# The second half's convolution taps without TensorE, and with only TensorE in the text's order

## The chip, the cores and the metric

One core of a Trainium2 chip runs the whole program. The metric is the time of one execution on the device in microseconds, the median of three runs: 2355.17 us (2353.74 to 2355.51) for the kernel before. The profile comes from one more execution with the profiler on, which took 2358.65 us. The engines are TensorE (PE), VectorE (DVE), ScalarE (ACT), GpSimd (POOL) and SyncE (SP), which issues the DMAs.

## What is computed

Two layers on an input of 1024 positions by 1024 channels. The first layer's mixer is attention, the second's is a Conformer convolution module; behind each mixer comes a feed-forward network with a short convolution (width 3). The change touches the Conformer module, whose core in the reference is:

```
u = h @ w_pw1 + b_pw1
a, g = jnp.split(u, 2, axis=-1)
u = a * jax.nn.sigmoid(g)
u = causal_dwconv(u, w_dw) + b_dw        # 31 taps, each channel by itself
u = rms_norm(u, ln_g)
u = jax.nn.silu(u)
return u @ w_pw2 + b_pw2
```

Each channel has 31 tap weights, and each output position is the sum of 31 shifted products.

## The kernel before

The module runs in two halves of 512 positions, h = 0 and 1. A half has eight tiles `ct` of 128 channels; channels lie across the partitions. All large products are three matmuls on a high and a low part of each operand (`whi`, `wlo` for weights, `hthi`, `htlo` for activations; lines 354 to 356), so each weight block that is loaded (`raw`) is split first: ScalarE makes `whi`, GpSimd or VectorE `wlo`.

For a tile, `glu` (line 1122) gives four weight pieces of 12 matmuls into two PSUM banks (`pw`); then `gate` makes `sg` on ScalarE and `u` on VectorE. `u` has two buffers of 30 + 512 columns. `taps_of` (line 1169) sums the taps:

- ScalarE multiplies the windows of the first `N_POOL` = 10 taps (`pacc`, then nine `prod`), and GpSimd adds them into `pacc`;
- VectorE takes the other taps one after the other into a PSUM tile `cacc` (line 1191), 21 of them;
- `end` adds both into `y` (line 1203). `square` then adds y squared into `sqa` (ScalarE and GpSimd).

In the second half, tiles 4, 5 and 6 (`PE_TILES`) are different: behind their `gate`, `on_pe` (line 1159) has ScalarE make four diagonal matrices `dg` from the tap weights, and TensorE multiplies them with windows of `u` in full float32 (line 1167). So four taps of these tiles are in `cacc` before VectorE begins, and VectorE takes 17.

`first` (line 1219) interleaves this: between groups of three taps it gives out pieces that hold matmuls, by a count (`beat`, `GATES`, `BEAT`) of how much VectorE work has gone out. Such pieces are the next tile's `glu` and fillers. In the second half the fillers are first `rest0`, the closing product of the first half (`dn` sums), with a norm of its four blocks of rows `turned` into the stream (ScalarE squares, GpSimd `ss`, VectorE `hn`, TensorE transposes `nps`, ScalarE `hthi`, VectorE `htlo`), and then `T.early` (`first = T.early(1, keep1, w_up)`), parts of the next up projection (`e` sums, each stored through a copy `ev` on ScalarE).

PSUM has six banks of the pool `up` for `pw`, `dn`, `e` and these `nps`, and two of the pool `t` for `cacc`, column sums and others.

When the taps of the half are done, `norm` (`squares`, `spread`) takes the column sums `ssps` of `sqa` on TensorE, makes the root on GpSimd (`r`), a diagonal `dg` on VectorE and spreads it with a matmul `rb`; then each `y` is scaled, goes through Silu, is split and feeds the closing product `dn`.

The order within an engine is either that of the program's text or one that a scheduler chooses before the program is built, with each instruction's place fixed from then on: every engine works through its own queue in order and waits at its head. `T.order` (line 236) opens a region; with no argument all engines are in the text's order, with `T.order(PE)` TensorE alone is, and the scheduler places the others. Before the change, `T.order()` without argument holds from the end of the first up projection to the start of the second.

Of the kernel before, what the change touches and what calls it, by code (L numbers as in the profile page):

```python
# [9 lines left out]
F32 = mybir.dt.float32  # L10
F32R = mybir.dt.float32r
BF16 = mybir.dt.bfloat16
AF = mybir.ActivationFunctionType
# [4 lines left out]
P = 128  # L18
# [31 lines left out]

N_POOL = 10
ROW_BUFS = 8
PE_TAPS = 4
PE_TILES = (4, 5, 6)
GATES = (2, 1)
BEAT = (3.3, 3.6)
LAG = 3
# [57 lines left out]
class Trunk:  # L115
# [993 lines left out]
    def conv(self, xs, xd, h, ht, w_pw1, los, taps, vec, w_pw2, halo, after):  # L1109


        nc = self.nc
        C = taps.shape[1]
        H = C - 1
        n_pool = N_POOL
        wv = w_pw1.rearrange("(k p) n -> p k n", p=P)
        st = {}
        us = {}
        ys = {}
        accs = {}  # L1120

        def glu(ct):
            pss = [None, None]
# [29 lines left out]
                for q in range(2):  # L1153
                    yield piece(s, q)
            yield Piece(gate, vector=1)
            if h == 1 and ct in PE_TILES:
                yield Piece(lambda: on_pe(ct))

        def on_pe(ct):

            dg = self.part("dg")
            acc = accs[ct] = self.pst.tile([P, 512], F32, tag="t", name=self.n("cacc"))
            for i in range(PE_TAPS):
                j = n_pool + i
                d = dg[:, i * P : (i + 1) * P]
                nc.scalar.activation(d, self.ident, AF.Copy, scale=taps[:, j, ct : ct + 1])
                nc.tensor.matmul(acc, d, us[ct][:, j : j + 512], start=i == 0, stop=i == PE_TAPS - 1)  # L1167

        def taps_of(ct):
            begun = h == 1 and ct in PE_TILES  # L1170
            own = n_pool + (PE_TAPS if begun else 0)
            nv = C - own
            t = {}
            tap = lambda j: taps[:, j, ct : ct + 1]

            def some(i0, i1):
                if i0 == 0:
                    t["u"] = us.pop(ct)
                    t["acc"] = accs.pop(ct) if begun else self.pst.tile([P, 512], F32, tag="t", name=self.n("cacc"))
                    t["pacc"] = self.part("pacc")  # L1180
                    t["done"] = 0
                u, acc, pacc = t["u"], t["acc"], t["pacc"]
                win = lambda j: u[:, j : j + 512]
                if i0 == 0:
                    nc.scalar.activation(pacc, win(0), AF.Identity, bias=vec[:, 2, ct : ct + 1], scale=tap(0))
                for i in range(i0, i1):
                    j = own + i
                    if i == 0 and not begun:
                        nc.vector.tensor_scalar(acc, win(j), tap(j), None, op0=ALU.mult)
                    else:  # L1190
                        nc.vector.scalar_tensor_tensor(acc, win(j), tap(j), acc, op0=ALU.mult, op1=ALU.add)  # L1191
                    while t["done"] < min(n_pool - 1, (n_pool - 1) * (i + 1) // (nv - 2)):
                        t["done"] += 1
                        p = self.part("prod")
                        nc.scalar.activation(p, win(t["done"]), AF.Copy, scale=tap(t["done"]))  # L1195
                        nc.gpsimd.tensor_tensor(pacc, pacc, p, op=ALU.add)  # L1196
# [117 lines left out]
def trunk(ctx, tc, a):  # L1314
    nc = tc.nc
    T = Trunk(ctx, tc)
# [28 lines left out]
    taps, vec = tabs[2]  # L1345
# [165 lines left out]
    def conv(h):  # L1511
        return T.conv(xs, xds[1], h, hc, w_pw1, pwlo, taps, vec, a["conv_w_pw2"][0], halo,
                      normer(grows, keep1, True))
# [4 lines left out]
    PE = mybir.EngineType.PE  # L1518

    def pieces():  # L1520
# [20 lines left out]
        yield from down1  # L1541
        yield from turned(rest0)
        main1, norm1, rest1 = conv(1)
        fill = [rest0]
        main1 = main1(fill)
        yield fetch(grows, a["ffn_norm_g"][1])
# [6 lines left out]
        first = T.early(1, keep1, w_up)  # L1553
        fill.append(first)
        yield from main1
        keep1["vector"] = True
        yield from some(first, 5)
        yield from some(norm1, 1)
# [17 lines left out]
        for d in downs:  # L1576
            yield from d

    T.trace(pieces())


# [23 lines left out]
```

## Time and profile before

| what | us |
|---|---|
| median of three runs | 2355.17 |
| profiled execution | 2358.65 |
| its span | 2356.9 |
| TensorE busy | 2270.7 (96%) |
| VectorE busy | 1648.0 (70%) |
| ScalarE busy | 1359.7 (58%) |
| GpSimd busy | 1402.2 (59%) |

The slices of the profile show the whole span in 40 parts; the second half's taps lie from about 1481 to 1674 us. Busy shares are means over stages with different limits, so the windows, the waits and the timeline of that stretch are to be read. An instruction is named by its line, output and inputs; `cacc<-u,dg` is a tap on TensorE, `cacc<-u,ctaps,cacc` one on VectorE.

### The profile page before, as it was taken

The numbers are of one execution on the slowest core, as the hardware profiler recorded it, in microseconds if no ns is written. First come the engines' busy times: TensorE is split into PE (matmuls) and PEld (weight loads), VectorE is DVE, ScalarE is ACT, GpSimd is POOL, SyncE is SP. The second block draws the span as 40 slices with busy tenths as digits, with TensorE's granted clock in tenths as the row PEclk, the third lists the DMA queues.
The fourth block names the chain that finished last, engine by engine and source line by source line (L and its number), as shares of the span: only waits on it lengthen the run. The fifth ranks groups of instructions, "written<-read, shape, count | busy, mean of one in ns | idle before, by whom it ended". The sixth has DMA issues, their size and how long they took to land.

```text
span 2356.9 us, 35332 instructions
## 1 busy us (share of the span) xinstructions
PE 2270.7 (96%) x11306; PEld 1934.8 (82%) x11306; DVE 1648.0 (70%) x2740; ACT 1359.7 (58%) x2844; POOL 1402.2 (59%) x1187
## 2 busy tenths in 40 slices
PE   7899999999999999999999999978999999999998
PEld 7899999997878887778778887856787888888887
DVE  5577777777378999997337985885738999993222
ACT  5566666666255666666455665555635666664443
POOL 3445545444018988884454895765634999965543
PEclk9999999998999999999999999999999999999999
DMA  4222322143155556666888777533555545466664
GB/s 144 64 79 79 81 77 77 57 166 131 69 176 184 155 161 213 200 198 200 285 273 291 235 251 264 176 110 112 183 180 170 155 152 156 153 220 208 216 206 155
DMA packets 366842, 392.64 MB, mean 167 GB/s; under 512 B 26416, under 2 KB 245312, under 8 KB 366656
## 3 DMA queue, kind: packets, MB, share of 16 engines
q1 hardware_dynamic: 366656, 390.38, 52.1%
q8 instruction: 89, 1.46, 0.2%
q14 instruction: 97, 0.79, 0.1%
HBM read 299.78 MB, written 82.12 MB: 162 GB/s over the span
## 4 chain that ended last, share of the span: by engine, by line
PE 44%; DVE 18%; issue 5%; ACT 3%; DMA 2%; POOL 2%; SPq 0%; DVEq 0%; ACTq 0%; POOLq 0%
DVE acc L580 9%; PE dn L355 7%; PE dn L356 7%; PE dn L354 7%; PE pw L354 2%; PE pw L356 2%; PE pw L355 2%; DVE cacc L1191 2%; PE e L356 1%; PE e L354 1%; PE e L355 1%; ACT acc L584 1%; PE y L354 1%; PE y L355 1%; PE y L356 1%
## 5 line engine op out<-in xcount | busy, mean ns | idle before, releaser
L349 POOL TENSOR_TENSOR wlo<-raw,whi 128x512 fp32r<-128x512 f32 (+1 forms) x305 | 443.0, 1454 | 270.1 <-ACT whi L348 237.2
L348 ACT CAST whi<-raw 128x512 fp32r<-128x512 f32 (+2 forms) x497 | 302.7, 633 | 248.3 <-PE dn L355 159.2
L349 DVE TENSOR_TENSOR wlo<-raw,whi 128x512 fp32r<-128x512 f32 (+1 forms) x192 | 149.5, 783 | 236.8 <-ACT whi L348 221.3
L349 POOL TENSOR_TENSOR wlo<-s,whi 128x512 fp32r<-128x512 f32 x176 | 258.7, 1480 | 66.8 <-ACT whi L348 66.6
L354 PE MATMUL dn<-whi,whi 128*128 128x512 f32 x704 | 276.1, 392 | 1.8 <-ACT whi L348 1.3
L355 PE MATMUL dn<-wlo,whi 128*128 128x512 f32 x704 | 275.2, 391 | 0.9 <-POOL wlo L349 0.9
L356 PE MATMUL dn<-whi,wlo 128*128 128x512 f32 x704 | 275.3, 391 | 0.0
L1191 DVE SCALAR_TENSOR_TENSOR cacc<-u,ctaps,cacc 128x512 f32<-128x512 f32 x311 | 235.0, 756 | 21.9 <-PE cacc L1167 11.5
L1196 POOL TENSOR_TENSOR pacc<-pacc,prod 128x512 f32<-128x512 f32 x144 | 190.1, 1320 | 87.2 <-ACT prod L1195 80.7
L354 PE MATMUL y<-bhi,whi 128*128 128x512 f32 x528 | 207.2, 392 | 6.6 <-DVE u L638 5.2
L356 PE MATMUL y<-bhi,wlo 128*128 128x512 f32 x528 | 205.6, 389 | 0.0
L355 PE MATMUL y<-blo,whi 128*128 128x512 f32 x528 | 205.5, 389 | 0.0
L171 POOL TENSOR_SCALAR ss<-ss 128x4 f32<-128x4 f32 (+1 forms) x96 | 22.8, 238 | 298.5 <-ACT hn L191 156.3
L354 PE MATMUL pj<-whi,hthi 128*128 128x384 f32 (+1 forms) x512 | 178.1, 349 | 5.3 <-DVE zf L824 3.6
L356 PE MATMUL pj<-whi,htlo 128*128 128x384 f32 (+1 forms) x512 | 177.5, 347 | 0.0
L355 PE MATMUL pj<-wlo,hthi 128*128 128x384 f32 (+1 forms) x512 | 176.5, 345 | 0.7 <-DVE wlo L349 0.7
L914 POOL TENSOR_SCALAR x<-x,nm 128x896 f32<-128x896 f32 (+7 forms) x128 | 101.0, 794 | 107.0 <-DVE nm L913 75.3
L558 POOL TENSOR_TENSOR s<-raw,raw 128x512 f32<-128x512 f32 x88 | 124.6, 1416 | 63.7 <-DMA raw<-in_ffn_w_up_dram 35.7
L354 PEld LDWEIGHTS dn<-whi,whi 128*128 128x128 f32 x704 | 132.9, 189 | 30.3 <-ACT whi L348 1.7
L355 PEld LDWEIGHTS dn<-wlo,whi 128*128 128x128 f32 x704 | 132.9, 189 | 29.1 <-POOL wlo L349 1.2
L356 PEld LDWEIGHTS dn<-whi,wlo 128*128 128x128 f32 x704 | 132.9, 189 | 27.6
L584 ACT ACTIVATE acc<-acc 128x512 f32<-128x512 f32 x88 | 55.7, 633 | 166.2 <-DVE acc L580 164.9
(224 smaller groups left out, 6442.8 us busy)
## 6 DMA issues: line engine op xcount, KB each, us to landing
raw<-in_ffn_w_up_dram SPq DMA_DIRECT2D x240, 256.0 KB
raw<-in_ffn_w_down_dram SPq DMA_DIRECT2D x176, 256.0 KB
raw<-actd SPq DMA_DIRECT2D x152, 256.0 KB
raw<-in_conv_w_pw_dram SPq DMA_DIRECT2D x96, 256.0 KB
actd<-acc SPq DMA_DIRECT2D x76, 256.0 KB
wlo<-pwlo SPq DMA_DIRECT2D x64, 256.0 KB
raw<-in_fox_w_in_dram SPq DMA_DIRECT2D x64, 192.0 KB
xd<-x SPq DMA_DIRECT2D x24, 512.0 KB
```

The costliest lines, as they stand in the source:

```text
L171: nc.gpsimd.tensor_scalar(ss, ss, 1.0 / n, EPS, op0=ALU.mult, op1=ALU.add)
L348: self.nc.scalar.copy(hi, raw)
L349: (self.nc.vector if vector else self.nc.gpsimd).tensor_tensor(lo, raw, f32(hi), op=ALU.subtract)
L354: nc.tensor.matmul(out, lh, rh, start=start, stop=False, skip_group_check=more)
L355: nc.tensor.matmul(out, lh, rl, start=False, stop=False, skip_group_check=more)
L356: nc.tensor.matmul(out, ll, rh, start=False, stop=stop, skip_group_check=more)
L558: nc.gpsimd.tensor_tensor(st[o], *(st[m].rearrange("p a b -> p (a b)") if m[0] == "a" else st[m] for m in ((y, x) if o == "s4" else (x, y) ...
L580: nc.vector.scalar_tensor_tensor(acc[:, j:], ps[:, : 512 - j], tap[2 - j], acc[:, j:], op0=ALU.mult, op1=ALU.add)
L584: nc.scalar.activation(acc, acc, AF.Silu)
L914: nc.gpsimd.tensor_scalar(X[:, :L], X[:, :L], nm[:, 2:3], 1.0, op0=ALU.mult, op1=ALU.mult)
L1191: nc.vector.scalar_tensor_tensor(acc, win(j), tap(j), acc, op0=ALU.mult, op1=ALU.add)
L1196: nc.gpsimd.tensor_tensor(pacc, pacc, p, op=ALU.add)
```

## The change

`on_pe` is taken out with its two constants, so every tile of both halves has 21 taps on VectorE and ten on ScalarE and GpSimd. And a region `T.order(PE)` is opened ahead of the second half's taps and closed with `T.order()` behind them: within it only TensorE keeps the text's order.

```diff
--- before.py
+++ after.py
@@ -50,8 +50,6 @@
 
 N_POOL = 10
 ROW_BUFS = 8
-PE_TAPS = 4
-PE_TILES = (4, 5, 6)
 GATES = (2, 1)
 BEAT = (3.3, 3.6)
 LAG = 3
@@ -1117,7 +1115,6 @@
         st = {}
         us = {}
         ys = {}
-        accs = {}
 
         def glu(ct):
             pss = [None, None]
@@ -1153,30 +1150,16 @@
                 for q in range(2):
                     yield piece(s, q)
             yield Piece(gate, vector=1)
-            if h == 1 and ct in PE_TILES:
-                yield Piece(lambda: on_pe(ct))
-
-        def on_pe(ct):
-
-            dg = self.part("dg")
-            acc = accs[ct] = self.pst.tile([P, 512], F32, tag="t", name=self.n("cacc"))
-            for i in range(PE_TAPS):
-                j = n_pool + i
-                d = dg[:, i * P : (i + 1) * P]
-                nc.scalar.activation(d, self.ident, AF.Copy, scale=taps[:, j, ct : ct + 1])
-                nc.tensor.matmul(acc, d, us[ct][:, j : j + 512], start=i == 0, stop=i == PE_TAPS - 1)
 
         def taps_of(ct):
-            begun = h == 1 and ct in PE_TILES
-            own = n_pool + (PE_TAPS if begun else 0)
-            nv = C - own
+            nv = C - n_pool
             t = {}
             tap = lambda j: taps[:, j, ct : ct + 1]
 
             def some(i0, i1):
                 if i0 == 0:
                     t["u"] = us.pop(ct)
-                    t["acc"] = accs.pop(ct) if begun else self.pst.tile([P, 512], F32, tag="t", name=self.n("cacc"))
+                    t["acc"] = self.pst.tile([P, 512], F32, tag="t", name=self.n("cacc"))
                     t["pacc"] = self.part("pacc")
                     t["done"] = 0
                 u, acc, pacc = t["u"], t["acc"], t["pacc"]
@@ -1184,8 +1167,8 @@
                 if i0 == 0:
                     nc.scalar.activation(pacc, win(0), AF.Identity, bias=vec[:, 2, ct : ct + 1], scale=tap(0))
                 for i in range(i0, i1):
-                    j = own + i
-                    if i == 0 and not begun:
+                    j = n_pool + i
+                    if i == 0:
                         nc.vector.tensor_scalar(acc, win(j), tap(j), None, op0=ALU.mult)
                     else:
                         nc.vector.scalar_tensor_tensor(acc, win(j), tap(j), acc, op0=ALU.mult, op1=ALU.add)
@@ -1541,6 +1524,7 @@
         yield from down1
         yield from turned(rest0)
         main1, norm1, rest1 = conv(1)
+        yield T.order(PE)
         fill = [rest0]
         main1 = main1(fill)
         yield fetch(grows, a["ffn_norm_g"][1])
@@ -1553,6 +1537,7 @@
         first = T.early(1, keep1, w_up)
         fill.append(first)
         yield from main1
+        yield T.order()
         keep1["vector"] = True
         yield from some(first, 5)
         yield from some(norm1, 1)
```

What this does to the queues, in rows of the built programs. In VectorE's queue before, where the norm's first rows come (`cacc_17486` and `u_17483` are tile 3, `u_17631` is tile 4, `nps` and `htlo` the first two blocks of the norm):

```order
L436 TENSOR_TENSOR x_16632<-x_16632,dn_17036 128x512
L1191 SCALAR_TENSOR_TENSOR cacc_17486<-u_17483,ctaps,cacc_17486 128x512 x15
L201 SCALAR_TENSOR_TENSOR hn_17556<-x_16629,ss_17555,rows_16833 128x512
L201 SCALAR_TENSOR_TENSOR hn_17556<-x_16629,ss_17555,rows_16835 128x512
L1145 SCALAR_TENSOR_TENSOR u_17631<-pw_3605_17503,cvec,sg_17629 128x512
L323 TENSOR_TENSOR htlo_3603_17498<-nps_17644,hthi_3601_17496 128x4x128
L323 TENSOR_TENSOR htlo_3604_17499<-nps_17651,hthi_3602_17497 128x4x128
L201 SCALAR_TENSOR_TENSOR hn_17625<-x_16629,ss_17624,rows_16833 128x512
L201 SCALAR_TENSOR_TENSOR hn_17625<-x_16629,ss_17624,rows_16835 128x512
L1191 SCALAR_TENSOR_TENSOR cacc_17486<-u_17483,ctaps,cacc_17486 128x512 x3
L1203 TENSOR_TENSOR y_17085<-cacc_17486,pacc_17487 128x512
```

The same place after (`cacc_17301` is tile 2, `u_17486` and `cacc_17489` tile 3):

```order
L434 TENSOR_TENSOR x_16632<-x_16632,dn_17039 128x512
L199 SCALAR_TENSOR_TENSOR hn_17559<-x_16629,ss_17558,rows_16836 128x512
L199 SCALAR_TENSOR_TENSOR hn_17559<-x_16629,ss_17558,rows_16838 128x512
L1174 SCALAR_TENSOR_TENSOR cacc_17301<-u_17280,ctaps,cacc_17301 128x512
L199 SCALAR_TENSOR_TENSOR hn_17628<-x_16629,ss_17627,rows_16836 128x512
L199 SCALAR_TENSOR_TENSOR hn_17628<-x_16629,ss_17627,rows_16838 128x512
L199 SCALAR_TENSOR_TENSOR hn_17661<-x_16632,ss_17660,rows_16836 128x512
L199 SCALAR_TENSOR_TENSOR hn_17661<-x_16632,ss_17660,rows_16838 128x512
L1174 SCALAR_TENSOR_TENSOR cacc_17301<-u_17280,ctaps,cacc_17301 128x512
L199 SCALAR_TENSOR_TENSOR hn_17661<-x_16632,ss_17702,rows_16836 128x512
L199 SCALAR_TENSOR_TENSOR hn_17661<-x_16632,ss_17702,rows_16838 128x512
L1142 SCALAR_TENSOR_TENSOR u_17486<-pw_3564_17310,cvec,sg_17484 128x512
```

The instructions `hn` of all four blocks now stand among the last taps of tile 2 and ahead of `u` of tile 3; before, they stood behind 15 taps of tile 3, and the later three each behind the transposes of the block before.

In TensorE's queue before, behind the last product `pw` of tile 4:

```order
L355 MATMUL pw_3619_17569<-htlo_3417_16564,whi_17432 128x512
L356 MATMUL pw_3619_17569<-hthi_3415_16562,wlo_17433 128x512
L1167 MATMUL cacc_17635<-u_17631,dg_17634 128x512 x4
L210 MATMUL nps_17644<-ident,hn_17556 128x128 x4
L210 MATMUL nps_17651<-ident,hn_17556 128x128 x4
L210 MATMUL nps_17673<-ident,hn_17625 128x128 x4
L210 MATMUL nps_17680<-ident,hn_17625 128x128 x4
L354 MATMUL pw_3643_17694<-hthi_3414_16561,whi_17456 128x512
```

And after:

```order
L353 MATMUL pw_3619_17572<-htlo_3417_16564,whi_17435 128x512
L354 MATMUL pw_3619_17572<-hthi_3415_16562,wlo_17436 128x512
L208 MATMUL nps_17643<-ident,hn_17559 128x128 x4
L208 MATMUL nps_17650<-ident,hn_17559 128x128 x4
L352 MATMUL pw_3638_17666<-hthi_3414_16561,whi_17459 128x512
```

The four tap matmuls are gone, the transposes of the first block follow the `pw` at once, and the 12 `pw` matmuls that begin in the last row stand before those of the second.

In ScalarE's queue after, where tile 5 begins (`sg_17861`, `u_17863`, `pacc_17918` are tile 5, `u_17634` is tile 4, `ev` frees a bank of an `e` sum):

```order
L1139 ACTIVATE sg_17861<-pw_3658_17779,cvec 128x512
L521 COPY ev_17879<-e_3677_17866 128x512
L1178 ACTIVATE prod_17889<-u_17634,ctaps 128x512
L521 COPY ev_17907<-e_3683_17894 128x512
L1168 ACTIVATE pacc_17918<-u_17863,cvec,ctaps 128x512
L1178 ACTIVATE prod_17923<-u_17863,ctaps 128x512
L1141 COPY u_18113<-halo 128x30
L98 CAST whi_17997<-raw_17731 128x512
L521 COPY ev_17938<-e_3669_17834 128x512
L1178 ACTIVATE prod_17949<-u_17863,ctaps 128x512
L1178 ACTIVATE prod_17974<-u_17863,ctaps 128x512
L1178 ACTIVATE prod_17979<-u_17863,ctaps 128x512
```

The second `ev` of `e_3669` stands behind `pacc_17918`, which reads `u_17863`. In this order products of two tiles follow each other, and copies `ev` stand among them. Besides, two `e` pieces (24 matmuls) of the up projection stand among the taps or before the closing product that stood in the second up projection before: the count in `first` gives out more fillers, since VectorE has more taps.

## Rows read from the trace of the kernel before

**Rows 1.** Windows: us; busy of PE, PEld, DVE, ACT, POOL; granted clock; DMA; GB/s.

```profile
1450.00:1555.00 105.00, 96.85 (x438) 78.62 (x436) 86.04 (x120) 63.21 (x114) 69.04 (x58) 1.00 0.58 193
1555.00:1640.00 85.00, 65.32 (x250) 46.19 (x251) 55.50 (x74) 41.52 (x78) 42.78 (x36) 0.90 0.34 112
1640.00:1720.00 80.00, 76.97 (x331) 62.10 (x330) 50.70 (x67) 45.53 (x80) 53.05 (x40) 0.98 0.60 194
...
1700.00:1720.00 20.00, 18.08 (x71) 14.21 (x71) 5.61 (x9) 10.69 (x19) 10.51 (x9) 0.91 0.70 247
```

**Rows 2.** Waits of TensorE, 1430 to 1740: us in total, times, longest.

```profile
PE cacc L1167 <- DVE u L1145: 16.5, 3, 8.2
PE nps L210 <- DVE hn L201: 9.7, 6, 2.2
```

**Rows 3.** Window of line 1167 alone: PE busy, weight loads, clock, DMA, GB/s.

```profile
1540.00:1640.00 100.00, 16.70 (x24) 6.49 (x24) 0.91 0.32 105
```

**Rows 4.** Waits of VectorE, 1481.5 to 1674.2, as rows 2.

```profile
DVE u L1145 <- ACT sg L1142: 13.8, 2, 12.8
DVE cacc L1191 <- PE cacc L1167: 11.5, 2, 5.9
DVE htlo L323 <- ACT hthi L322: 6.8, 1, 6.8
DVE y L1203 <- POOL pacc L1196: 6.0, 3, 3.9
DVE wlo L349 <- ACT whi L348: 5.7, 2, 3.4
```

**Rows 5.** Timeline of VectorE in the taps: start, us, instruction, count.

```profile
1503.03 15.80 DVE L1191 SCALAR_TENSOR_TENSOR cacc<-u,ctaps,cacc 128x512 f32<-128x512 f32 x20
...
1544.79 11.84 DVE L1191 SCALAR_TENSOR_TENSOR cacc<-u,ctaps,cacc 128x512 f32<-128x512 f32 x15
```

**Rows 6.** Timeline of TensorE: start, us, instruction, count, [idle before and what ended it].

```profile
1558.77 5.61 PE L1167 MATMUL cacc<-u,dg 128*128 128x512 f32 x8 [8.24 <-DVE u L1145]
...
1567.48 1.32 PE L210 MATMUL nps<-ident,hn 128*128 128x128 f32 x8 [2.22 <-DVE hn L201]
...
1681.24 0.49 PE L354 MATMUL e<-hthi,whi 128*128 128x512 f32 x1
...
1689.55 1.02 PE L1265 MATMUL rb<-dg,ones 128*128 128x512 f32 x2
...
1697.14 0.50 PE L354 MATMUL dn<-whi,hthi 128*128 128x512 f32 x1 [1.11 <-ACT hthi L1273]
```

**Rows 7.** Window of VectorE alone: busy us (instructions), clock, DMA, GB/s.

```profile
1481.00:1674.14 193.14, 156.54 (x208) 0.96 0.41 130
```

**Rows 8.** Timeline of VectorE around the last tap.

```profile
1672.85 0.68 DVE L349 TENSOR_TENSOR wlo<-raw,whi 128x512 fp32r<-128x512 f32 x1
1673.45 0.69 DVE L1203 TENSOR_TENSOR y<-cacc,pacc 128x512 f32<-128x512 f32 x1
1675.83 4.54 DVE L349 TENSOR_TENSOR wlo<-raw,whi 128x512 fp32r<-128x512 f32 x3 [1.69 <-ACT whi L348]
```

**Rows 9.** Timeline of GpSimd behind the last tap.

```profile
1674.88 1.29 POOL L1217 TENSOR_TENSOR sqa<-sqa,sq 128x512 f32<-128x512 f32 x1 [5.88 <-ACT sq L1216]
...
1676.82 1.30 POOL L558 TENSOR_TENSOR s<-raw,raw 128x512 f32<-128x512 f32 x1 [0.65 <-DVE wlo L349]
...
1684.52 1.29 POOL L349 TENSOR_TENSOR wlo<-s,whi 128x512 fp32r<-128x512 f32 x1
```

**Rows 10.** Timeline of VectorE at the start of the up projection.

```profile
1819.64 0.69 DVE L628 TENSOR_TENSOR u<-y,p 128x512 f32<-128x512 f32 x1 [3.33 <-PE y L356]
```

**Rows 11.** Three tiles, 1481.5 to 1674.2: count, ns min/median/max, first and last start.

```profile
L349 DVE TENSOR_TENSOR wlo<-raw,whi x12: 683/1018/1418, 1589.4 to 1672.9; 128x512 fp32r<-128x512 f32 x12
...
L201 DVE SCALAR_TENSOR_TENSOR hn<-x,ss,rows x8: 737/756/1755, 1556.5 to 1579.6; 128x512 f32<-128x512 f32 x8
...
L1191 DVE SCALAR_TENSOR_TENSOR cacc<-u,ctaps,cacc x151: 742/756/757, 1482.6 to 1672.2; 128x512 f32<-128x512 f32 x151
```

## The prediction

> **What bounds the kernel now.** I began with the windows around the second half's taps [rows 1]. The reader is to see that TensorE is busy nearly all of 1450 to 1555 us, then only 65.32 of the 85 us from 1555 to 1640, at a granted clock of 0.90, and again nearly all of the time to 1720. VectorE is at 86.04 of 105 us in the first stretch and at 55.50 of 85 in the second: there both engines wait. The waits of TensorE [rows 2] name two lines: its tap matmuls wait 16.5 us for `u`, and the transposes `nps` wait 9.7 us for `hn`. Both `u` and `hn` come from VectorE. The tap matmuls themselves take 16.70 us [rows 3]. VectorE waits in turn [rows 4]: 11.5 us for those tap matmuls, 6.8 us for `hthi`, which is made from the transposes that stand behind them, 6.0 us for the adds of GpSimd (`pacc`), 5.7 us for `whi` from ScalarE, 1.0 us for `sg` (the other 12.8 of that row is the wait before the stage). So the two engines hold each other in turns, and neither is the bound alone. The order explains why: in the text's order 15 taps (11.84 us) stand on VectorE before the first `hn` and the next `u` [rows 5], while TensorE has been idle for 8.24 us [rows 6].
>
> **The change on VectorE.** From the start of the first `u` to the end of the last `y` are 193.14 us with 208 instructions [rows 7]. The waits of rows 4 in it are 11.5 + 6.8 + 6.0 + 5.7 + 1.0 = 31.0 us. The change gives VectorE 12 taps more, four for each of tiles 4, 5 and 6. Twenty taps take 15.80 us [rows 5], 0.79 each with the gap, so 9.5 us. With no wait left the stage would take 193.1 - 31.0 + 9.5 = 171.6 us, and the last `y` would end 21.5 us earlier, at 1652.6.
>
> Which waits go? The 11.5 us go with the matmuls. The 6.8 us go too: the order puts the eight `hn` in front of `u` of tile 3, so that the transposes find their inputs when TensorE comes to them. That is 18.3 us. The other 12.7 (`pacc`, `whi`, `sg`) depend on how the scheduler has ordered ScalarE and GpSimd; the bounds are that all stay or none. Going through the queues, I find the products of a tile on ScalarE well ahead of the `y` that needs them, with one place that is tight: the `pacc` of tile 5 waits on ScalarE for `u` of tile 5 and has a product of tile 4 just before it. I keep 3 us. The last `y` then ends at 1655.6, 18.5 us earlier; the bounds are 8.8 and 21.5.
>
> **The change on TensorE.** It loses 16.70 us of tap matmuls and, by the above, most of the 26.2 us of waits in rows 2. In the order of after, 384 matmuls and 32 transposes stand from the first transposes to the column sums (`ssps`). The 36 matmuls from 1681.24 to `rb` at 1689.55 took 0.23 us each, and eight transposes 1.32 [rows 6]: 384 x 0.23 + 4 x 1.32 = 93.6 us. In the trace this work can begin at 1558.77 - 8.24 = 1550.5, so TensorE is through at 1644.1. The sums need the last `sqa`, which ends 2.0 us behind the last `y` (1674.88 + 1.29 against 1673.45 + 0.69) [rows 8, 9], so at 1657.6. TensorE has 13.5 us to spare, and VectorE becomes the bound of the stage. The 12 scaled copies that ScalarE loses cost nothing there, since it is busy for half of that stretch [rows 1]. On the DMA queue the two loads of the norm's gains move up a few places; no wait of rows 2 or 4 ends with a DMA, so I take nothing, in either direction.
>
> **Behind the last `y`.** Before, `rb` came 15.4 us after it (1689.55 against 1674.14). TensorE set that: three `e` pieces stood between. Now it is the way through GpSimd. A load of a `w_up` block for its sums `s` needs a buffer that a `wlo` of VectorE frees; in the order of after this `wlo` stands behind the last `y`, before it stood ahead of it. The first `wlo` behind `y` began at 1675.83, and three took 4.54, so it ended about 3.2 us after `y`. From the buffer's freeing (1672.85 + 0.68) to `s` (1676.82) are 3.3 us with the load, and from `s` to `rb` 12.7, of which one `wlo` of GpSimd (1.29, at 1684.52) now stands behind `r` [rows 6, 8, 9]. Sum: 3.2 + 3.3 + 11.4 = 17.9, or 2.5 us more than before. `rb` is 16.0 us earlier. Behind it come three `e` pieces before the first `dn` instead of two: 36 x 0.23 + 1.0 for `rb` = 9.3 us, where 7.6 passed before (with a wait of 1.11) [rows 6]. The first `dn` is 14.3 us earlier.
>
> From there TensorE has 24 matmuls less to do, since two `e` pieces have moved up into the taps: 24 x 0.23 = 5.5 us. They stood among the first pieces of the up projection, in front of work that VectorE prepares. VectorE had 3.33 us to spare there [rows 10], and two `wlo` of about 1.0 each move with the pieces; that covers 5.3 of the 5.5. I take 1.0 us of loss; the bounds are 0 and 2.2.
>
> TensorE now waits some 6 us ahead of `rb` and some more ahead of `ssps`. From 1700 to 1720 us, with 1.9 us idle, the granted clock is 0.91 [rows 1]: if that is the lower of the two levels, 1.2 GHz, for a part of the time, it is 3.6 us at half rate, 1.8 us lost. I take this once; the bounds are 0 and 3.6.
>
> **The sum.** 14.3 + 5.5 - 1.0 - 1.8 = 17.0 us less. The profiled execution took 2358.65 us, 3.5 above the median of the runs, 2355.17. So 2342 us in a profile of this kind, and 2338 as the median.
>
> **A rule against it.** The `hn` (eight) took from 0.737 to 1.755 us each and the twelve `wlo` from 0.683 to 1.418, while the 151 taps lie between 0.742 and 0.757 [rows 11]. `hn` and `wlo` read two operands in SBUF, a tap one (its sum lies in PSUM). The Trainium skill (SBUF — State Buffer, Who interferes with whom) says that a VectorE instruction with two SBUF inputs and a GpSimd instruction that reads SBUF shut each other out for a whole instruction. By that rule, and the trace agrees, closer packing of the two engines costs VectorE time, up to the price of the second rival; by the rows as they stand it costs nothing more than now.
>
> **The rivals.**
> - *The 12.7 us stay.* ScalarE and GpSimd still come late in the scheduler's order. For it: every engine takes its queue in order, and a product behind a copy that waits is late as before. Against it: in the new order the products stand early, and the tap matmuls no longer push them back. It gives 9.7 us less gain: 7.3, or 2348 us.
> - *VectorE and GpSimd block each other more.* All of `hn` at 1.755 and all of `wlo` at 1.418: 8 x (1.755 - 0.756) + 12 x (1.418 - 1.018) = 12.8 us more on the engine that now bounds: 4.2 us faster, 2351 us, and half of that 2345. For it: rows 11. Against it: most of what the order mixes are taps, which take the same beside a busy GpSimd. The rule above is the Trainium skill's (SBUF — State Buffer).
> - *Everything fits.* None of the 3.0, 1.0 and 1.8 us is lost and `wlo` runs at 0.683 (12 x 0.335 = 4.0): 26.8 us, 2328 us.
> - *TensorE runs out of PSUM banks* (slower). Six banks hold the `pw` and `e` sums. The copy `ev` that frees an `e` bank stands on ScalarE behind `pacc` of the next tile, which waits for `u`, which stands on VectorE behind 20 taps, 15.8 us. If each of tiles 5, 6 and 7 holds TensorE for that long, it loses 47.4 us; 13.5 are spare, the gain of 17.0 goes, and 16.9 are added: 2372 us. It decides from 31 us of such waits on. For it: the order on ScalarE shows just this row of instructions. Against it: by my count of the banks TensorE is caught for 4 to 10 us in all.
>
> **How the numbers follow.** The forecast has 0.60 (its own range 2331 to 2344), the waits that stay 0.15, the blocking 0.08, the full fit 0.05, the banks 0.12, of which 0.07 is slower and 0.05 about no change. About 0.2%, or 4.7 us, is what a measurement here can tell from no change. Faster: 0.60 + 0.15 + 0.05 + half of the blocking, 0.04 = 0.84; within: 0.04 + 0.05 = 0.09; slower: 0.07. The range 2327 to 2350 takes in the full fit, the waits that stay and half of the blocking.
>
> **What would show it.** In the profile after: no idle time of TensorE that `u` or `hn` ended; VectorE busy without a gap from the first `u` to the last `y`, some 175 us; a wait of TensorE before `ssps` or `rb`, ended by GpSimd or VectorE; a first `dn` about 14 us earlier. It is wrong if VectorE still waits over 10 us for `pacc` or `whi`, or if TensorE's longest waits end with ScalarE's `ev`.

## The result and the profile after

The changed kernel takes 2334.89 us (median of four runs, 2333.51 to 2335.16); the kernel before takes 2355.28 beside it. The ratio is 0.9914, with a 95% interval of 0.9896 to 0.9931: faster by 20.4 us, or 0.9%. Forecast were 2338 us and a range from 2327 to 2350. The profiled execution of the changed kernel took 2333.51 us, its span is 2331.8.

Executions begin to differ long before the second half's taps (the first `u` of the half starts at 1481.0 us before and at 1478.8 after), so I count from that `u`. From there to the end of the span were 875.9 us and are 853.0: 22.9 less. To the end of the last `y` were 193.1 and are 169.7. A profile is one execution, and that of the kernel before (2358.65 us) lay 3.4 us above its median, so such differences come out larger than the 20.4 us between the medians.

The windows of the same three stretches, and of 1700 to 1720 [rows 1]:

```profile
1450.00:1555.00 105.00, 102.28 (x465) 84.18 (x466) 83.36 (x123) 64.61 (x111) 70.16 (x60) 0.98 0.67 216
1555.00:1640.00 85.00, 77.11 (x335) 63.02 (x334) 82.59 (x112) 53.54 (x95) 66.20 (x51) 0.94 0.44 139
1640.00:1720.00 80.00, 72.45 (x308) 58.16 (x307) 30.38 (x44) 31.97 (x56) 33.18 (x27) 0.96 0.51 166
1700.00:1720.00 20.00, 20.00 (x90) 16.55 (x89) 4.17 (x7) 4.35 (x7) 5.88 (x5) 1.00 0.35 102
```

VectorE (the third busy time) went from 55.50 to 82.59 of 85 us in the middle stretch: it is full. TensorE (the first) still has 8 us free there. The waits of TensorE from 1430 to 1740 say where, then those of VectorE in its stage [rows 2, 4] (us in total, times, longest):

```profile
PE e L352 <- ACT ev L521: 7.8, 1, 7.8
PE rb L1248 <- DVE dg L1244: 5.7, 1, 5.7
...
PE nps L208 <- DVE hn L199: 2.1, 1, 2.1
...
```

```profile
DVE u L1142 <- ACT sg L1139: 17.3, 3, 14.5
DVE x L434 <- PE dn L354: 2.8, 2, 1.4
DVE wlo L347 <- ACT whi L346: 0.5, 2, 0.3
DVE y L1186 <- POOL pacc L1179: 0.4, 1, 0.4
```

Line 1167 and its 16.70 us [rows 3] are gone. No wait for `u` is left on TensorE, and the one for `hn` lies ahead of the first `u` (in the first half's stream, as 2.1 of rows 2 did). Of VectorE's 17.3 us for `sg`, 14.5 lie before the stage; within it 2.8 + 2.8 + 0.5 + 0.4 = 6.5 us of waits remain of 31.0. TensorE's two long waits are new: 7.8 us for an `ev`, and 5.7 ahead of `rb`.

VectorE's stage as a whole [rows 7], and its taps with what follows the last `y` [rows 5, 8], in two fences; the stage's row gives its length, busy time and instructions, the timeline start, us, instruction and count:

```profile
1478.80:1648.45 169.65, 159.69 (x220) 0.96 0.49 150
```

```profile
1566.34 9.96 DVE L1174 SCALAR_TENSOR_TENSOR cacc<-u,ctaps,cacc 128x512 f32<-128x512 f32 x15
...
1590.01 11.82 DVE L1174 SCALAR_TENSOR_TENSOR cacc<-u,ctaps,cacc 128x512 f32<-128x512 f32 x15
...
1647.76 0.69 DVE L1186 TENSOR_TENSOR y<-cacc,pacc 128x512 f32<-128x512 f32 x1
1650.14 1.70 DVE L347 TENSOR_TENSOR wlo<-raw,whi 128x512 fp32r<-128x512 f32 x2 [1.69 <-ACT whi L346]
...
1662.63 2.89 DVE L1244 TENSOR_SCALAR dg<-ident,r 128x128 f32<-128x128 f32 x4 [7.70 <-POOL r L170]
```

The reader is to see two groups of 15 taps of the same shape, one of 9.96 us and one of 11.82. In the first the taps of two tiles alternate; in the second all go into one `cacc`. I come back to this. On GpSimd behind the last `y` [rows 9], and on TensorE [rows 6]:

```profile
1649.20 1.29 POOL L1200 TENSOR_TENSOR sqa<-sqa,sq 128x512 f32<-128x512 f32 x1 [8.01 <-ACT sq L1199]
1654.43 1.56 POOL L556 TENSOR_TENSOR s<-raw,raw 128x512 f32<-128x512 f32 x1 [3.94 <-DMA raw<-in_ffn_w_up_dram]
...
1661.57 1.02 POOL L170 TENSOR_TENSOR r<-r,mhalf 128x4 f32<-128x4 f32 x1
```

```profile
1579.91 0.79 PE L352 MATMUL e<-hthi,whi 128*128 128x512 f32 x1 [7.85 <-ACT ev L521]
...
1650.54 1.05 PE L1236 MATMUL ssps<-ones,sqa 128*128 128x1 f32 x8
...
1665.57 2.08 PE L1248 MATMUL rb<-dg,ones 128*128 128x512 f32 x2 [5.70 <-DVE dg L1244]
...
1677.01 0.39 PE L352 MATMUL dn<-whi,hthi 128*128 128x512 f32 x1
```

The load that `s` needs lands late, `r` stands behind the sums, and TensorE waits for `rb`: that is the way the prediction went through the queues. `rb` starts 17.1 us after the last `y` (forecast 17.9). TensorE reaches `ssps` without a wait just as `sqa` is ready (1649.20 + 1.29): it has no time to spare. What it waited for at 1572 to 1580 us stands on ScalarE:

```profile
1575.72 0.22 ACT L1141 COPY u<-halo 128x30 f32<-128x30 f32 x1 [3.24 <-DVE cacc L1174]
1576.92 0.63 ACT L1199 ACTIVATE sq<-y 128x512 f32<-128x512 f32 x1 [0.98 <-DVE y L1186]
...
1579.30 0.56 ACT L521 COPY ev<-e 128x512 f32<-128x512 f32 x1
```

The `ev` stands behind a copy into a `u` buffer that taps of VectorE still read, behind a square that needs a `y`, and behind three products. Behind each of TensorE's two long stalls its matmuls start 0.43 us apart instead of 0.23, while the granted clock has fallen:

```profile
1575.00:1580.00 5.00, 0.09 (x1) 0.50 0.17 50
1580.00:1590.00 10.00, 10.00 (x34) 0.75 0.44 157
...
1665.00:1672.00 7.00, 6.43 (x16) 0.62 0.18 69
```

(Windows of TensorE alone: busy, instructions, granted clock, DMA, GB/s.) 0.50 is the lower of the two levels, 1.2 GHz. After the stall from 1572 to 1580 us twelve matmuls ran at it, 12 x 0.20 = 2.4 us lost; later `rb` took 2.08 us where it had taken 1.02, and the matmuls behind it started 0.43 us apart up to 1670.

### The profile page after: what moved, and what is told of

The parts are those of the page before. It is cut to its first block, busy times and chain, and to the rows that moved or that the text cites. A ratio compares the mean times of both kernels' runs of the same rounds, so it can differ in the third digit from the quotient of the medians.

```text
span 2331.8 us, 35304 instructions
## 1 busy us (share of the span) xinstructions
PE 2253.5 (97%) x11282; PEld 1927.3 (83%) x11282; DVE 1650.9 (71%) x2751; ACT 1355.8 (58%) x2832; POOL 1403.7 (60%) x1188
## 3 DMA queue, kind: packets, MB, share of 16 engines
q8 instruction: 89, 1.46, 0.3%
## 4 chain that ended last, share of the span: by engine, by line
PE 49%; DVE 15%; issue 4%; ACT 4%; DMA 2%; POOL 1%; SPq 0%; DVEq 0%; ACTq 0%; POOLq 0%
DVE acc L578 8%; PE dn L353 7%; PE dn L352 7%; PE dn L354 7%; PE pw L352 2%; PE pw L353 2%; PE pw L354 2%; PE y L352 2%; PE e L352 2%; PE e L354 2%; PE e L353 2%; PE y L353 2%; PE y L354 2%; ACT acc L582 1%; PE z L352 1%
```

## The experiments

The theory that I went in with (A): what counts is VectorE's queue, where `hn` and `u` stood behind 15 taps; the removed taps add to it. Rivals: the removed taps do it all (B), the order does it all (C). All runs are listed once here; the stages are read from each profile: from the first `u` to the end of the last `y`, from that `u` to the start of `rb`, and from `rb` to the end of the span, in us. Each ratio is to runs of the kernel before that were taken beside it; the stages are from one execution each, which can lie some microseconds off the median (2328.25 against 2334.87 us in the kernel with only VectorE ordered anew).

| kernel | median | ratio to before (95%) | `u` to `y` | `u` to `rb` | `rb` to end |
|---|---|---|---|---|---|
| before | 2355.28 | 1 | 193.2 | 208.6 | 667.4 |
| changed | 2334.89 | 0.9914 (0.9896 to 0.9931) | 169.7 | 186.8 | 666.2 |
| taps removed, text's order | 2339.85 | 0.9929 (0.9912 to 0.9945) | 174.2 | 191.4 | 665.2 |
| order alone | 2342.91 | 0.9942 (0.9927 to 0.9957) | 174.5 | 191.8 | 666.7 |
| changed, VectorE in text's order | 2344.67 | 0.9952 (0.9935 to 0.9969) | 177.4 | 194.5 | 665.2 |
| changed, only VectorE ordered anew | 2334.87 | 0.9903 (0.9885 to 0.9921) | 169.0 | 186.2 | 666.0 |
| tap matmuls without `u` | 2347.00 | 0.9969 (0.9956 to 0.9981) | 184.5 | 199.9 | 667.4 |
| changed, two sums per tile | 2331.06 | 0.9902 (0.9887 to 0.9918) | 162.5 | 179.7 | 665.8 |
| taps removed, two sums per tile | 2335.18 | 0.9916 (0.9902 to 0.9929) | 172.9 | 190.1 | 668.2 |
| changed, 9 `raw`, 13 general buffers | 2319.23 | 0.9844 (0.9831 to 0.9858) | 167.6 | 182.5 | 659.1 |
| changed, 13 general buffers | 2327.79 | 0.9879 (0.9865 to 0.9892) | 169.9 | 186.7 | 663.0 |
| changed, 10 `raw`, 12 general | 2326.86 | 0.9876 (0.9861 to 0.9891) | 166.2 | 181.2 | 665.6 |
| two sums, 9 `raw`, 13 general | 2318.24 | 0.9837 (0.9824 to 0.9851) | 164.2 | 179.1 | 660.4 |
| before, 9 `raw`, 13 general | 2347.76 | 0.9967 (0.9955 to 0.9980) | 192.8 | 208.2 | 664.1 |

### The first part alone

```diff
--- changed kernel
-        yield T.order(PE)
...
-        yield T.order()
```

> The first part of the change alone: the taps of tiles 4, 5 and 6 leave TensorE, every engine keeps the text's order. Theory A (it is VectorE's place for `hn` and `u` in its queue that counts, and the removed taps only add to it): VectorE loses 11.5 us of waits for the tap matmuls and takes 9.5 us of taps for them; `hn` still stands behind 15 taps of tile 3, so TensorE still stands idle for some 8 us ahead of the transposes and VectorE still waits for `hthi`. The last `y` is 2 to 9 us earlier, the time 3 to 9 us shorter than before: 2346 to 2352 us. Theory B (the taps on TensorE were the brake, the order is an extra): at least 16 us shorter, 2339 or less.

2339.85 us, 15 below the kernel before. Theory A is wrong here: by the medians three quarters of the gain need no new order. B's bound is just missed. The interval of the ratio overlaps that of the changed kernel, so that the order adds something to this is shown by the stage in the traces (174.2 against 169.7 us), not by the time. TensorE's waits from 1480 to 1700, and VectorE's from 1478 to 1659:

```profile
PE nps L208 <- DVE hn L199: 11.8, 3, 6.8
...
```

```profile
DVE u L1142 <- ACT sg L1139: 14.9, 3, 12.8
DVE wlo L347 <- ACT whi L346: 0.8, 1, 0.8
DVE y L1186 <- POOL pacc L1179: 0.6, 1, 0.6
DVE htlo L321 <- ACT hthi L320: 0.2, 1, 0.2
```

As expected, the `hn` still come late and TensorE stands for them, 11.8 us. But it doesn't matter: VectorE's own waits have gone almost entirely (2.1 + 0.8 + 0.6 + 0.2 = 3.7 us of 31.0), among them 6.6 of the 6.8 for `hthi` that I had credited to the order, and most of those for `pacc` and `whi` that I had left open. VectorE runs through, and it bounds.

### The second part alone

```diff
--- before
+        yield T.order(PE)
         fill = [rest0]
...
         yield from main1
+        yield T.order()
```

> The second part alone: the taps of tiles 4, 5 and 6 stay on TensorE, and only TensorE is in the text's order in the second half's taps. Theory A: the eight `hn` stand ahead of `u` of tile 3, so the 9.7 us of waits for `hn` and the 6.8 us for `hthi` go; the tap matmuls (16.7 us) and part of the waits for them stay. TensorE then has about 105 us of work from 1550, and VectorE some 176 us: the time is 8 to 14 us shorter than before, 2341 to 2347. Theory C (the order alone does it all): 2338 or less. Theory B (the removed taps do it all): within 4 us of before.

2342.91 us, 12 less: in A's range; C falls, and so does B, by which this had to stay within 4 us of before. TensorE's waits from 1480 to 1700:

```profile
PE cacc L1167 <- ACT dg L1166: 7.2, 2, 4.8
PE cacc L1167 <- DVE u L1145: 2.8, 1, 2.8
...
```

With `u` early, 2.8 us of waits for it remain of 16.5; now the diagonal matrices of ScalarE are late. The two parts give 15.0 and 12.0 us alone and 20.4 together. From the first `u` to the last `y` either part alone is 19 us shorter, both are 23.5. VectorE's waits from 1478 to 1659 in this run:

```profile
DVE u L1145 <- ACT sg L1142: 17.5, 4, 14.5
DVE wlo L349 <- ACT whi L348: 7.9, 4, 4.5
DVE cacc L1191 <- PE cacc L1167: 5.6, 1, 5.6
DVE x L436 <- PE dn L356: 2.8, 2, 1.4
```

Less the 14.5 for `sg` ahead of the stage and 1.7 for `whi` behind it, 17.6 us stand against 31.0 (2.8 of them new, for `dn`), so the order alone takes 13.4; the first part took 27.3, both together take 24.5. They overlap: neither `hthi` nor `pacc` is waited for in either run for more than 0.6 us. The rest of what the order brings alone is shorter work, on which more below.

### VectorE in the text's order, and VectorE alone in the scheduler's

```diff
--- changed kernel
-        yield T.order(PE)
+        yield T.order(PE, mybir.EngineType.DVE)
```

```diff
--- changed kernel
-        yield T.order(PE)
+        yield T.order(PE, mybir.EngineType.Activation, mybir.EngineType.Pool, mybir.EngineType.SP)
```

> The changed kernel with VectorE, too, in the text's order in the second half's taps; ScalarE, GpSimd and the DMA queues are still placed by the scheduler. Theory A: the gain of the order lies in VectorE's queue, so this falls back to what the first part alone gives, within 3 us of it, 2344 to 2352. The rival (the gain lies in ScalarE's and GpSimd's queues, where products and `ev` are placed): 2339 or less. Besides, no two tiles' taps alternate on VectorE here, so all taps should take 0.79 us with their gap, and none 0.66.

> The changed kernel with VectorE alone placed by the scheduler; ScalarE, GpSimd and the DMA queues are in the text's order as TensorE is. Theory A: it keeps nearly all of the gain, 2334 to 2341. The rival (ScalarE and GpSimd had to be placed anew as well): it loses at least half of it, 2345 or more, and the wait that takes the place is VectorE's for `hthi` or for `pacc`, or TensorE's for `hn`, since the squares and `ss` that lead to `hn` stand late on ScalarE and GpSimd.

2344.67 and 2334.87 us; the intervals of the two ratios do not overlap. With VectorE in the text's order nothing of the order's gain is left: the time is 4.8 us above that of the first part alone (A had said within 3), and the stage is 3.2 us longer, at the same order of VectorE. As expected, the 146 taps that follow one of their own tile all start 0.79 us after it. One place shows where: the eight `hn` take longer there (tile `hn`, first of the first part alone, then of this kernel; ns min/median/max):

```profile
L199 DVE SCALAR_TENSOR_TENSOR hn<-x,ss,rows x8: 740/744/1753, 1559.3 to 1575.2; 128x512 f32<-128x512 f32 x8
```

```profile
L199 DVE SCALAR_TENSOR_TENSOR hn<-x,ss,rows x8: 739/1484/1772, 1556.6 to 1578.0; 128x512 f32<-128x512 f32 x8
```

In sum 7.65 and 10.17 us, 2.5 of the 3.2. With VectorE alone placed by the scheduler, all of the gain is kept. So of the engines set free by `T.order(PE)` only VectorE's queue pays; in this A holds for the part that the order brings, and the products on ScalarE and GpSimd, of which the prediction was afraid, are as good in the text's order.

### What the order saves: distance between taps

In the trace of the first part alone 15 taps into one tile take 11.83 us. In the changed kernel those that alternate between two tiles take 9.96 (above): a tap starts 0.66 us after an instruction that wrote another tile, 0.79 after one that wrote its own. By the orders of the built programs, 146 of 168 taps follow a tap of their own tile in the text's order, 95 in the changed kernel: 51 x 0.13 = 6.6 us. The stage is 4.5 us shorter. The waits are 2.8 us longer, the `wlo` 2.7 (14.38 against 11.65), the `hn` 1.7 shorter: -6.6 - 1.7 + 2.8 + 2.7 = -2.8, so 1.7 of the 4.5 are not accounted for. In the order alone the pairs fall from 134 to 102 of 156 taps, 4.2 us, and the `hn` take 5.9 us instead of 8.6. To test it, two sums for every tile:

```diff
+                    if h == 1:
+                        t["odd"] = self.pst.tile([P, 512], F32, tag="t", name=self.n("codd"))
...
                     j = n_pool + i
+                    acc = t["odd"] if h == 1 and i % 2 else even_acc
-                    if i == 0:
+                    if i == 0 or (i == 1 and h == 1):
...
                 nc.vector.tensor_tensor(y, t["acc"], t["pacc"], op=ALU.add)
+                if h == 1:
+                    nc.vector.tensor_tensor(y, y, t["odd"], op=ALU.add)
```

> The changed kernel, with the 21 taps of a tile summed in turns into two PSUM tiles (`cacc`, `codd`) in the second half, and one more add for each `y`. In the traces so far a tap that follows a tap into the same tile starts 0.79 us after it, one that follows another tile's instruction 0.66. In the changed kernel 95 of 168 taps follow one into the same tile; here none does. 95 x 0.13 = 12.4 us less, eight more adds at some 0.7 are 5.8 more: VectorE needs 6 to 7 us less for the stage. Theory D (VectorE bounds the changed kernel's stage, as predicted): the last `y` 6 us earlier, the time 3 to 6 us below the changed kernel, 2329 to 2332. Rival E (TensorE is level with VectorE when it comes to the column sums, and holds it up): within 2 us of the changed kernel, and TensorE shows no longer wait ahead of `ssps`.

> The first part alone (no taps on TensorE, all engines in the text's order) with the two PSUM tiles for the taps in turn. 146 of 168 taps followed one into the same tile there, so VectorE needs 146 x 0.13 = 19.0 - 5.8 = 13 us less. If the distance between taps into one tile is what the scheduler's order takes out by mixing two tiles' taps, this reaches the changed kernel's time without any new order: 2330 to 2336. Rival: the `hn` that stand behind 15 taps keep TensorE waiting (12.6 us in the first part's run), TensorE becomes the bound, and the time stays within 4 us of the first part's 2339.9.

The second kernel shows the distance best, since its order is the text's: VectorE's timeline at the end of a tile (start, us, instruction, count):

```profile
1490.76 0.75 DVE L1177 SCALAR_TENSOR_TENSOR codd<-u,ctaps,codd 128x512 f32<-128x512 f32 x1
1491.42 0.75 DVE L1177 SCALAR_TENSOR_TENSOR cacc<-u,ctaps,cacc 128x512 f32<-128x512 f32 x1
1493.07 0.69 DVE L1189 TENSOR_TENSOR y<-cacc,pacc 128x512 f32<-128x512 f32 x1 [0.91 <-POOL pacc L1182]
1493.80 0.69 DVE L1191 TENSOR_TENSOR y<-y,codd 128x512 f32<-128x512 f32 x1
1494.40 0.75 DVE L1142 SCALAR_TENSOR_TENSOR u<-pw,cvec,sg 128x512 f32<-128x512 f32 x1
```

Taps in turn start 0.66 us apart. The second add waits for the first (0.73 from start to start), the `u` behind it does not (0.60). So the distance is shown, in SBUF as in PSUM. What it is worth is less: in this kernel 13 us less work became 1.3 us in the stage (174.2 to 172.9). VectorE's waits in it grow from 3.7 to 13.9 us (7.8 for `pacc`, since GpSimd's adds are now too late for the taps, 4.6 for `sg`, 1.5 for `whi`), its `hn` take 2.0 us more, and TensorE still waits 11.8 us for them. By the ratios to before, 0.9916 against 0.9929, the gain can't be told from none. The median of 2335.18 lies in the range of the first expectation, but the trace speaks against it. The rival is half right: TensorE does wait for `hn`, but VectorE's longest waits are for GpSimd, which neither named.

In the changed kernel with two sums the stage is 7.2 us shorter, as expected, and TensorE now waits at the column sums:

```profile
1647.99 1.05 PE L1241 MATMUL ssps<-ones,sqa 128*128 128x1 f32 x8 [2.27 <-POOL sqa L1205]
```

That speaks for theory D: VectorE bounds the stage. TensorE came earlier here as well, since no wait for an `ev` is left in this run; but in the changed kernel VectorE waits only 0.9 us in all from that wait of TensorE to its last `y`, so it was not the 7.8 us for the `ev` that set the stage. The median, 2331.06, lies in D's range, but the intervals of the two ratios (0.9887 to 0.9918 and 0.9896 to 0.9931) overlap; so the shorter stage is shown and the gain in the whole time is not.

### The mutual wait

```diff
--- before
+            for i in range(PE_TAPS):
+                d = dg[:, i * P : (i + 1) * P]
-                nc.tensor.matmul(acc, d, us[ct][:, j : j + 512], start=i == 0, stop=i == PE_TAPS - 1)
+                nc.tensor.matmul(acc, d, dg, start=i == 0, stop=i == PE_TAPS - 1)
```

> The kernel before, whose 12 tap matmuls on TensorE read the diagonal tile `dg` in place of `u`; the sums of tiles 4, 5 and 6 so lack four taps. TensorE has the same 16.7 us of matmuls, VectorE the same 17 taps in these tiles, but TensorE no longer stands still at the head of its queue until `u` comes. Theory F (it was the mutual wait, `u` behind 15 taps and all of TensorE's queue behind `u`, that cost the time): the 16.5 us of waits go, part comes back as waits for `hn`; 8 to 14 us below the kernel before, 2341 to 2347. Rival G (the 16.7 us of work on TensorE cost it): within 4 us of before.

2347.00 us, 8.9 less by the medians: at the lower end of F, and against G. It is no exact price of the mutual wait: for `dg` of ScalarE TensorE now waits 7.3 us, since the first of these matmuls needs all four matrices, and the matmuls take 14.49 us instead of 16.70. VectorE's waits in the stage:

```profile
...
DVE cacc L1193 <- PE cacc L1169: 8.9, 2, 5.2
DVE y L1205 <- POOL pacc L1198: 6.0, 3, 3.9
DVE wlo L349 <- ACT whi L348: 5.5, 2, 3.4
DVE htlo L323 <- ACT hthi L322: 0.4, 1, 0.4
```

The wait for `hthi` falls from 6.8 to 0.4 though no instruction of VectorE has moved: it came from TensorE, which stood at `u` with the transposes behind it. The 6.0 for `pacc` and 5.5 for `whi` stay as in the kernel before. Both go in the first part's run, where VectorE has 21 taps in place of 17 and ScalarE no `dg` to make; which of the two does it was not taken apart. With the order alone only the one for `pacc` goes.

### The way to `rb`, and a better version

```diff
--- changed kernel
-RAW_BUFS = 8
+RAW_BUFS = 9
-PART_BUFS = 14
+PART_BUFS = 13
```

> The changed kernel with nine buffers for loaded weights (`raw`) instead of eight and 13 instead of 14 of the general ones. Behind the last `y` the sums `s` of GpSimd wait for a load that needs a buffer which a `wlo` of VectorE frees, and `r`, `dg` and `rb` come behind it; TensorE stands idle for 5.7 us ahead of `rb`. If the buffer is the cause, `rb` comes 3 to 5 us earlier and the time falls by 2 to 5 us, to 2330 to 2333. Rivals: the load waits for another buffer or its place in the DMA queue, and nothing changes (2333 to 2336); or the lost general buffer makes products wait, and it is slower (over 2337).

2319.23 us, a ratio of 0.9844: far below every theory. GpSimd behind the last `y`, and `rb` on TensorE:

```profile
1644.63 1.29 POOL L1200 TENSOR_TENSOR sqa<-sqa,sq 128x512 f32<-128x512 f32 x1 [7.24 <-ACT sq L1199]
1645.88 1.75 POOL L556 TENSOR_TENSOR s<-raw,raw 128x512 f32<-128x512 f32 x1
```

```profile
1658.81 1.12 PE L1248 MATMUL rb<-dg,ones 128*128 128x512 f32 x2 [1.46 <-DVE dg L1244]
```

The sum `s` now follows `sqa` without the 3.94 us for the load, TensorE waits 1.46 us instead of 5.70, and `rb` runs at nearly its old length. But from the first `u` to `rb` only 4.3 us are gained, 2.2 of them behind the last `y`, and the time fell by 15.7, so three more runs:

> The changed kernel with 13 general buffers in place of 14, `raw` unchanged at eight. If the ninth `raw` buffer was the cause of the 16 us, this has the changed kernel's time or a little more, 2333 to 2339. Rival (the smaller general pool, by what the scheduler makes of it, was the cause): 2326 or less.

> The kernel before with nine `raw` buffers and 13 general ones. Theory H (behind the last `y` the load waits for a buffer only because the change has moved the `wlo` that frees it; in the kernel before TensorE came to `rb` late by itself): at `rb` nothing is gained, elsewhere as much as in the changed kernel, so 6 to 12 us less, 2344 to 2350. Rival I (the buffer helps the program the same in both kernels): 14 to 18 us less, 2338 to 2342.

> The changed kernel with ten `raw` buffers and 12 general ones. If loads that wait for a `raw` buffer are still in the way with nine, another few microseconds go: 2310 to 2317. Rival (with nine no load is late any more; what is left is TensorE's and VectorE's work): within 2 us of the nine buffers, 2317 to 2321, or above it if the products and squares now want general buffers.

```diff
--- the three, in this order: changed kernel, before, changed kernel
-RAW_BUFS = 8 / PART_BUFS = 14
+RAW_BUFS = 8 / PART_BUFS = 13
+RAW_BUFS = 9 / PART_BUFS = 13
+RAW_BUFS = 10 / PART_BUFS = 12
```

With 13 general buffers alone it is 2327.79, between the two ranges: by the medians 7.1 us of the 15.7 come from a smaller pool, which I had not thought of, and 8.6 from the ninth `raw` on top of it (nine with 14 general ones were not run). TensorE still waits 5.4 us ahead of `rb` there, so it is the ninth buffer that ends that wait. In the kernel before both together give 8.1 us, within H's range, and nothing of it between the first `u` and `rb` (208.2 against 208.6): there TensorE came late by itself. Ten and 12 are worse again, 2326.86; `rb` comes early there too (2.1 us of wait), but the stretch behind it is 6.5 us longer than with nine and 13. Between `rb` and the end the better kernels win 3 to 7 us, and why a general buffer less helps there (and how much of it lies ahead of the taps) was not found; the orders of the built programs differ from the first up projection on.

> The changed kernel with both: two PSUM tiles for a tile's taps in turn, and nine `raw` buffers with 13 general ones. The former shortened VectorE's stage by some 7 us in its trace, the latter the way from the last `y` to `rb` by 3 and the program by 16. If VectorE's stage still bounds, the two add: 2311 to 2316. Rival (TensorE is the bound of the stage by now, or the two give the same time twice): within 2 us of the nine buffers alone, 2317 to 2321.

2318.24 us with two sums and nine buffers together: the rival, no more than 1 us below the nine buffers alone. The stage is 3.4 us shorter in the trace, the way to the first `u` 1.7 longer and `rb` to the end 1.3; so neither of the rival's reasons is shown: TensorE waits 2.3 us at `ssps`, and the time won in the stage is lost elsewhere. The nine buffers are the version to keep, 16 us below the changed kernel, 36 below the one before.

## Why the prediction was right, and where not

**The direction and the mechanism** held in the main: the mutual wait was a cost (8.9 us went with it alone, though a wait for `dg` came in its place), and VectorE bounds the stage after. That the order was needed to end that wait did not hold, and what makes up the rest of the 15.0 us of the removal is not shown. One of the prediction's own signs of being wrong came true: TensorE's longest wait, 7.8 us, ends with ScalarE's `ev`.

**VectorE's stage.** Forecast were 174.6 us, measured 169.65. The step that failed is the price of the twelve taps, 12 x 0.79 = 9.5 us. All taps were charged at the distance of taps into one tile. Counted by pairs, before has 156 taps, 134 of them behind their own tile, after 168 and 95: 12 x 0.66 - 39 x 0.13 = 2.8 us. That is 6.7 less. The `hn` take 5.93 us instead of 8.63, 2.7 less, and the twelve `wlo` 14.38 instead of 12.14, 2.2 more. The rows of the two tiles [rows 11], count and ns min/median/max:

```profile
L199 DVE SCALAR_TENSOR_TENSOR hn<-x,ss,rows x8: 741/746/1121, 1536.8 to 1543.2; 128x512 f32<-128x512 f32 x8
```

```profile
L347 DVE TENSOR_TENSOR wlo<-raw,whi x12: 676/1250/1796, 1552.3 to 1634.3; 128x512 fp32r<-128x512 f32 x12
```

The waits that stay are 6.5 us, not 3. Together -6.7 - 2.7 + 2.2 + 3.5 = -3.7 of the -5.0; errors of both signs partly cancelled, which is luck.

**Which waits go, and by what.** The prediction gave 11.5 us to the matmuls, 6.8 to the order of `hn`, and left 12.7 open. The reasons did not hold: the removal alone takes 27.3 of the 31.0, the 6.8 included, with the `hn` where they were. The order alone takes 13.4, the 6.8 again among them. What I had read as two causes was one circle, TensorE at `u` and VectorE at `hthi`, and either part opens it.

**TensorE.** The work was sized well, the 13.5 us to spare were not there: 7.85 us went to the `ev`, some 2.4 to the half rate behind it, and 5.0 because VectorE was through earlier; TensorE came to `ssps` level with it. This is the rival of the PSUM banks at the size that the prediction counted for it (4 to 10 us), but by another way: the `ev` stood behind the copy into `u` and the square, not behind a `pacc`. It cost VectorE no more than 0.9 us of waits after it, and the sums of TensorE were not late; that is why this sign of being wrong did not decide.

**Behind `y`.** `rb` at 17.1 us against 17.9; the first `dn` 11.4 behind `rb` against 9.3, the 2.1 us being the half clock at `rb`. For the clock 1.8 us were put in, so this evens out. In the up projection [rows 10] TensorE waits 1.5 us for an `acc` of ScalarE where it waited 0.4, near the 1.0 that was put in; from the first `dn` to the end 5.0 us are gained, where 5.5 - 1.0 were forecast. From the first `u`, `rb` is 21.8 us earlier (forecast 16.0), `dn` 18.0 (14.3), the end 22.9 (17.0): the error of 5 us in the stage goes through to the end.

**The other rivals.** The 12.7 us did not stay. VectorE and GpSimd did not block each other more on balance: `wlo` was dearer, `hn` cheaper. Of the rivals the full fit is nearest in size, 26.8, but its reason did not hold: the `wlo` became dearer, and the waits and the half clock stayed.

## What to carry to other kernels

When two engines wait for each other in turns, the waits on both sides are one cost: give it out once, and test each edit alone before crediting it with "its" wait. On a full engine count the pairs of neighbours in the order, not only the instructions: a chain into one accumulator is dearer than two chains in turn; how much of that reaches the stage depends on what waits next (7.2 us in one kernel here, 1.3 in another). And after a bound has moved, look for the buffer that the next link waits for; here the wait at `rb` fell from 5.70 to 1.46 us with one more load buffer, while a general buffer less won several microseconds for a reason that was not found.

## What the runs showed of the hardware

- An instruction of VectorE that reads what the one before it wrote starts 0.13 us later than one that does not, for 128x512 float32: taps 0.79 and 0.66, adds 0.73 and 0.60, in PSUM and in SBUF. The taps last 0.75 us each, so one that depends on the tap before starts 0.04 us behind its end, and another 0.09 us ahead of it; whether the wait in the program or the engine itself sets this was not taken apart. The Trainium skill (VectorE: DVE Perf Modes, Rules for kernel authors) advises on chained operations: "Don't try to fuse for perf — DRAIN happens regardless. Minimize op *count*, not sems". Its DRAIN is the flush of the engine's pipeline behind an operation. Here the order counts as well as the number, by the 0.79 and 0.66 us above, and the measurement decides.
- With nine buffers five `wlo` of VectorE and the sums `s` of GpSimd run side by side, and both stretch. The `wlo` take 7.69 us in all, over twice the 0.69 that one takes in the changed kernel at the same place, and `s` up to 1.75 instead of 1.28:

```profile
1645.58 7.69 DVE L347 TENSOR_TENSOR wlo<-raw,whi 128x512 fp32r<-128x512 f32 x5 [1.69 <-ACT whi L346]
```

  Both read two operands in SBUF. This agrees in kind with the rule of the Trainium skill (SBUF — State Buffer, Who interferes with whom) which the prediction weighed: from the first `s` to the last, five instructions of GpSimd start 1.73 us apart on the mean (1645.88 to 1652.80), where in the changed kernel they start some 1.25 apart by themselves and a `wlo` and an `s` one after the other would be 0.69 + 1.28 = 1.97 us.
